# The first and last microseconds of a two-layer block: a weight piece multiplied in fp32, another first root, a second transposing of one chunk, smaller output pieces

## The chip, the cores and the metric

The kernel runs on one core of a Trainium2 chip. Its engines work beside each other: TensorE (PE, with its weight loads shown as PEld), VectorE (DVE), ScalarE (ACT), GpSimd (POOL) and SyncE (SP), which here only issues DMAs. The metric is the device time of one execution in microseconds (us); for the kernel before it is the median of three runs. One further execution was taken with the hardware profiler, and all durations come from that one.

## What is computed

Two layers over 256 tokens of width 1024, all in fp32. Each layer is a half-step feed-forward block, a mixer (a recurrent one in layer 0, an mLSTM in layer 1) and another half-step feed-forward block, each behind an RMS norm that is modulated by a condition vector c. Only the first block's entry and the final norm matter here:

```python
c_act = silu(c)
mod = (c_act @ ada_w[layer] + ada_b[layer]).reshape(1, 3, 3, D_MODEL)
h = rms_norm(x, norm_g[0, 0]) * (1 + mod[:, 0, 1]) + mod[:, 0, 0]
x = x + 0.5 * (1 + mod[:, 0, 2]) * (silu(h @ w_gate) * (h @ w_up)) @ w_down
...
return rms_norm(x, final_norm_g)
```

with `rms_norm(x, g) = x * rsqrt(mean(x * x) + 1e-6) * g`.

## The kernel before

**Layout.** The state x is held transposed, as 8 chunks of 128 channels by 256 tokens. A product has a 128x128 weight tile as its stationary operand and a 128x256 chunk as its moving one. To keep fp32 accuracy at the speed of the narrower type fp32r, each operand is split into a high part (rounded to fp32r) and a low part (the rest), and `multiply` makes three products: high by high, high by low, low by high.

**Weights.** `Weights` brings the weights in pieces of 8 tiles (128x1024, 512 KB) in the order of use. `_piece` (L88) issues a piece's DMA on SP's queue into one of four buffers `wraw`, makes the high part on ScalarE (L96 for the first two pieces, L100 for the others) and the low part on VectorE (L101). A buffer is free for the piece four later when both have read it. `behind` adds order among the instructions of one engine without a wait for data.

**The start (L171 to L212, L298 to L344, L521 to L594).** SP's queue brings x in two blocks of 128 tokens, `xn[:, 0]` and `xn[:, 1]`, then the rows of the modulation matrix in blocks of 512 KB (`ada`), the column vectors `cols` (biases, gains, filter taps) and the weight pieces. ACT's queue brings c. PE spreads c over 128 partitions (L200), ScalarE applies silu (`cact`). VectorE sums the squares of each token (L206). PE transposes x (L211) and ScalarE copies it (L212). `rsqrt_act` (L298) makes the root with ScalarE's Sqrt, which needs a table load, and one correction on VectorE; `spread` (L342) lays it over all partitions as a row. `ada_block` (L223) is one VectorE instruction that multiplies a block with `cact` and sums along the row, which gives 128 values of shift or scale; block 2k and block 2k+1 hold chunk k's shift and scale. b1 (L542) is the fixed part of the scale. Eight transposes (`WARM`, L530) keep PE at work until the first product.

Then the loop over chunks k (L548). Chunks 0 and 1 are modulated by `modulate_chunk` (L400): a VectorE product with scale and root (L404), ScalarE's high part (L406), VectorE's low part (L407). Chunks 2 to 7 are first multiplied by the root three at a time (L563) and then modulated on ScalarE (L566 to L570), the low part on VectorE (L571). For each chunk PE runs through 8 output tiles with gate and up, 16 weight tiles or two pieces, 48 products; results add up in 8 banks of PSUM. The two ada blocks of chunk k+1 are placed in the program behind the first tile of chunk k. A scheduler sets the order on each engine from priorities and from the orders that the kernel adds by hand (`add_manual_dep`, `issue_after`); each engine and each DMA queue then works strictly in its order.

**Beside it.** `dt_weights` (L654) loads a small matrix `wdt` over POOL's queue, for the mixer 200 us later, and splits it (L660, L661).

**The end (L1299 to L1315).** `rsqrt_act` makes the final root of the token sums; PE transposes x back (L1306) into four banks; ScalarE scales the first 128 tokens (L1312) and VectorE the second (L1314), 512 columns at a time, and each result of 256 KB goes out by its own DMA, three on SP's queue and one on ACT's.

Of the kernel before, what the change touches and what calls it, by code (L numbers as in the profile page):

```python
# [11 lines left out]
F32 = mybir.dt.float32  # L12
F32R = mybir.dt.float32r
I32 = mybir.dt.int32
AF = mybir.ActivationFunctionType
ALU = mybir.AluOpType
# [14 lines left out]
    ("ada_b", 6 * 24), ("norm_g", 6 * 8),  # L31
# [32 lines left out]
WARM = 8  # L64
# [8 lines left out]
class Weights:  # L73
# [14 lines left out]
    def _piece(self, i):  # L88
        nc = self.nc
        w = PIECE * P  # L90
        raw = self.raw_pool.tile([P, w], F32, tag="wraw", name=f"wraw{i}")
        nc.sync.dma_start(raw, self.src[i])
        hi, lo = (self.part_pool.tile([P, w], F32R, tag=f"{n}{'abc'[i % 3]}", name=f"{n}{i}") for n in ("whi", "wlo"))
        with self.tc.high_priority(offset=self.ahead):
            if i < 2:
                raw_hi = nc.scalar.copy(hi, raw)  # L96
                if i == 1:
                    self.tc.add_manual_dep(raw_hi.ins, self.first[1].ins.name, NOSYNC, reason="the first input first")
            else:
                raw_hi = nc.scalar.copy(hi, raw)  # L100
            self.last = nc.vector.tensor_tensor(out=lo, in0=raw, in1=hi.bitcast(F32), op=ALU.subtract)  # L101
        if i < 2:
            self.tc.add_manual_dep(self.last.ins, self.first[0].ins.name, NOSYNC, reason="the first input first")
        self.parts[i] = (hi, lo)
        self.splits[i] = (raw_hi, self.last)
        if i:
# [15 lines left out]
    def next(self):  # L122
        i, k = divmod(self.pos, PIECE)
        if k == 0:
            while self.made <= min(i + (self.LEAD if i >= 2 * NF0 - 3 else 1), NTILE // PIECE - 1):
                self._piece(self.made)
                self.made += 1
            self.parts.pop(i - 1, None)
            self.pump(i)
        self.pos += 1  # L130
        hi, lo = self.parts[i]
        return hi[:, k * P:(k + 1) * P], lo[:, k * P:(k + 1) * P]
# [3 lines left out]
def body(ctx: ExitStack, tc: tile.TileContext, a, out, dbg=None):  # L136
# [42 lines left out]
    cols = cst.tile([P, NCOL], F32, name="cols")  # L179
    xs_t = [xall[:, k, :] for k in range(ND)]  # L180
# [16 lines left out]
    cact = cst.tile([P, D], F32, name="cact")  # L197
    for i in range(2):
        b = mm_bank(f"c{i}")
        nc.tensor.matmul(b, ones[0:1, :], crow[:, 512 * i:512 * i + 512], start=True, stop=True)  # L200
        nc.scalar.activation(cact[:, 512 * i:512 * i + 512], b, AF.Silu)

    ss_in = fpool.tile([P, 2], F32, name="ss_in")
    for b in range(2):
        q = fpool.tile([P, D], F32, tag="xsq", name=f"xsq{b}")
        squares = nc.vector.scalar_tensor_tensor(out=q, in0=xn[:, b], scalar=1.0, in1=xn[:, b], op0=ALU.mult,  # L206
                                                 op1=ALU.mult, accum_out=ss_in[:, b:b + 1])
    for k in range(0, ND, 2):
        b = mm_bank(f"xT{k}")
        for i in range(4):  # L210
            nc.tensor.transpose(b[:, i * P:(i + 1) * P], xn[:, i % 2, (k + i // 2) * P:(k + i // 2 + 1) * P], ident)  # L211
        nc.scalar.copy(xall[:, k:k + 2, :], b.rearrange("p (k t) -> p k t", k=2))  # L212
# [68 lines left out]
    def rsqrt_small(v, shape, nm):  # L281
# [11 lines left out]
        nc.vector.scalar_tensor_tensor(out=w, in0=w, scalar=-0.5, in1=v, op0=ALU.mult, op1=ALU.mult)  # L293
        end = nc.vector.scalar_tensor_tensor(out=y, in0=w, scalar=1.5, in1=y, op0=ALU.add, op1=ALU.mult)
# [3 lines left out]
    def rsqrt_act(sums, nm):  # L298

        v = small.tile([P, 2], F32, tag="rs_v", name=f"rsv_{nm}")  # L300
        y = small.tile([P, 2], F32, tag="rs_y", name=f"rsy_{nm}")
        w = small.tile([P, 2], F32, tag="rs_w", name=f"rsw_{nm}")
        nc.vector.tensor_scalar(out=v, in0=sums, scalar1=1.0 / D, scalar2=EPS, op0=ALU.mult, op1=ALU.add)
        nc.scalar.activation(y, sums, AF.Sqrt, bias=eps, scale=1.0 / D)
        nc.vector.reciprocal(y, y)
        nc.vector.tensor_tensor(out=w, in0=y, in1=y, op=ALU.mult)
        nc.vector.scalar_tensor_tensor(out=w, in0=w, scalar=-0.5, in1=v, op0=ALU.mult, op1=ALU.mult)
        return y, nc.vector.scalar_tensor_tensor(out=y, in0=w, scalar=1.5, in1=y, op0=ALU.add, op1=ALU.mult)
# [62 lines left out]
    def multiply(dst, both, start, stop):  # L371

        wh, wl = W.next()
        m = nc.tensor.matmul(dst, wh, both[:, 0, :], start=start, stop=False, skip_group_check=True)  # L374
# [134 lines left out]
    def ffn(s, acc, fp, during=None):  # L509
# [11 lines left out]
        if s == 0:  # L521
# [7 lines left out]
            for _ in range(WARM):  # L529
                nc.tensor.transpose(warm[:, 0:P], xn[:, 0, 0:P], ident)  # L530
            banks = [mm_bank(f"gu0_{j}") if j < 4 else ax_bank(f"gu0_{j}", ("ax", "ax", "p", "q")[j - 4])
                     for j in range(NF0)]
# [7 lines left out]
            b1 = modp.tile([P, 8], F32, tag="gate", name="b1")  # L540
            o, g = COL["ada_b"], COL["norm_g"]
            plus = nc.vector.scalar_tensor_tensor(out=b1, in0=cols[:, o + 8:o + 16], scalar=1.0, in1=cols[:, g:g + 8],  # L542
                                                  op0=ALU.add, op1=ALU.mult)
            tc.add_manual_dep(plus.ins, second_ada.ins.name, NOSYNC, reason="the norm first")
# [3 lines left out]
            for k in range(ND):  # L548
                sc, sh = scales[0][:, k:k + 1], shifts[0][:, k:k + 1]
                gain, bias = cols[:, g + k:g + k + 1], cols[:, o + k:o + k + 1]  # L550
                if k < 2:
# [3 lines left out]
                    chain = modulate_chunk(0, k, pb if k == 0 else rs)  # L555
                    late = chain[2]
                    if k == 1:
                        W.behind(2, 1, chain[0])
                        W.behind(3, 0, chain[1])
# [18 lines left out]
                if k == 0:  # L578
                    W.first = chain
                    nc.scalar.copy(rs, pb)  # L580
                for j in range(NF0):
                    for i in range(2):
                        dst = banks[j][:, i * T:(i + 1) * T]

                        m = multiply(dst, h[k], k == 0 and i == 0, k == ND - 1)
# [4 lines left out]
                        if j == i == 0 and k + 1 < ND:  # L590
                            ada_block(2 * k + 2)
                            ada_block(2 * k + 3)
# [708 lines left out]
    rs, _ = rsqrt_act(sum_tokens(acc, "fin", "mm")[:, 0:2], "fin")  # L1301
# [6 lines left out]
    for lo in (0, 512):  # L1308
        for b in range(2):
            dst, src = res[:, b, lo:lo + 512], banks[2 * (lo // 512) + b]  # L1310
# [4 lines left out]
            (nc.scalar if b == 0 and lo else nc.sync).dma_start(out[b * P:(b + 1) * P, lo:lo + 512], dst)  # L1315
# [108 lines left out]
```

## Time and profile before

| | us |
|---|---|
| median of three runs (lowest, highest) | 1102.14 (1101.68, 1102.78) |
| the profiled execution's own time | 1102.35 |
| its span, first to last record | 1100.6 |
| busy PE, DVE, ACT in the span | 1086.5, 920.1, 642.5 |
| first product of the first block starts | 12.69 |
| last product of the last block starts | 1091.52 |
| first output DMA is issued | 1095.54 |

A line of the order of time gives start and length in us, engine, line of the code, operation, result and operands with their shapes, and in brackets how long the engine had been idle and what ended it. Neighbouring instructions of one kind are merged (x4); the length is then that of the group. A product's record lasts about 0.28 us while the next starts in less than half of that, since products are pipelined. The table of stretches gives busy times of PE, PEld, DVE, ACT and POOL, the granted clock, the share of the 16 DMA engines and GB/s.

### The profile page before, as it was taken

How to read it: one execution, taken by the hardware profiler on the slowest of the kernel's cores; microseconds unless marked ns; L12 is line 12 of the kernel's file. 1: busy time of each engine (PE TensorE's matmuls, PEld its weight loads, DVE VectorE, ACT ScalarE, POOL GpSimd, SP SyncE). 2: the span in 40 equal slices, each digit the busy share in tenths (PEclk: the TensorE clock that was granted, in tenths of full speed). 3: DMA queues.
4: the chain of work that ended last, by engine and by line, in shares of the span. 5: the costliest groups of instructions: out<-in, count | busy, mean ns of one | idle time of the engine just before them, and what ended most of it. 6: DMA issues, size and time to landing. Idle time of an engine off the chain costs nothing.

```text
span 1100.6 us, 23364 instructions
## 1 busy us (share of the span) xinstructions
PE 1086.5 (99%) x9350; PEld 1073.0 (97%) x9350; DVE 920.1 (84%) x1651; ACT 642.5 (58%) x1051; POOL 9.4 (1%) x29
## 2 busy tenths in 40 slices
PE   8999999999999999999999999999999999999997
PEld 7999999999999999999999999999999999999997
DVE  7999998999999899989699988869878868766552
ACT  5665555677986664554454554448776655544452
POOL 0000000000000000000000000010000000000000
PEclk9999999999999999999999999999999999999999
DMA  9989998556845489999848998963432665875551
GB/s 372 335 318 375 393 353 334 192 192 192 287 161 180 155 308 370 351 349 324 279 166 318 347 314 307 316 200 116 151 97 92 198 194 159 269 236 195 195 173 39
DMA packets 74990, 272.34 MB, mean 247 GB/s; under 512 B 8417, under 2 KB 8577, under 8 KB 74882
## 3 DMA queue, kind: packets, MB, share of 16 engines
q1 hardware_dynamic: 74304, 269.49, 70.1%
q8 instruction: 73, 1.20, 0.4%
q0 software_dynamic: 432, 1.10, 0.4%
q14 instruction: 35, 0.29, 0.1%
q10 hardware_dynamic: 146, 0.27, 0.1%
HBM read 269.77 MB, written 1.05 MB: 246 GB/s over the span
## 4 chain that ended last, share of the span: by engine, by line
PE 81%; DVE 13%; ACT 2%; issue 2%; DMA 1%; SPq 0%; DVEq 0%; ACTq 0%
PE gu L375 13%; PE gu L376 13%; PE gu L374 13%; PE od L374 10%; PE od L375 10%; PE od L376 10%; DVE wlo L101 4%; PE gu_f L436 1%; DVE xc L627 1%; PE gu_f L437 1%; PE gu_f L438 1%; DVE ada L232 1%; PE zz L375 1%; PE zz L376 1%; PE zz L374 1%
## 5 line engine op out<-in xcount | busy, mean ns | idle before, releaser
L101 DVE TENSOR_TENSOR wlo<-wraw,whi 128x1024 fp32r<-128x1024 f32 x366 | 445.6, 1221 | 94.4 <-ACT whi L100 92.5
L100 ACT CAST whi<-wraw 128x1024 fp32r<-128x1024 f32 x364 | 380.3, 1050 | 225.5 <-PE od L375 70.8
L375 PE MATMUL gu<-hb,whi 128*128 128x256 f32 x1312 | 361.1, 276 | 0.4 <-DVE hb L571 0.4
L376 PE MATMUL gu<-hb,wlo 128*128 128x256 f32 x1312 | 360.9, 276 | 0.0
L374 PE MATMUL gu<-hb,whi 128*128 128x256 f32 x1312 | 358.6, 277 | 0.8 <-ACT whi L96 0.5
L375 PEld LDWEIGHTS gu<-hb,whi 128*128 128x128 f32 x1312 | 246.3, 188 | 0.8 <-DVE hb L571 0.8
L376 PEld LDWEIGHTS gu<-hb,wlo 128*128 128x128 f32 x1312 | 246.3, 188 | 0.0
L374 PEld LDWEIGHTS gu<-hb,whi 128*128 128x128 f32 x1312 | 244.5, 188 | 1.8 <-ACT whi L96 0.7
L374 PE MATMUL od<-ph,whi 128*128 128x256 f32 x704 | 194.4, 276 | 0.0
L376 PE MATMUL od<-ph,wlo 128*128 128x256 f32 x704 | 194.4, 276 | 0.0
L375 PE MATMUL od<-ph,whi 128*128 128x256 f32 x704 | 194.4, 276 | 0.0
L232 DVE SCALAR_TENSOR_TENSOR ada<-ada,cact 128x1024 f32<-128x1024 f32 x144 | 175.2, 1218 | 0.9 <-DMA ada<-in_adaT_dram 0.9
L375 PEld LDWEIGHTS od<-ph,whi 128*128 128x128 f32 x704 | 132.2, 188 | 0.0
L376 PEld LDWEIGHTS od<-ph,wlo 128*128 128x128 f32 x704 | 132.2, 188 | 0.0
L374 PEld LDWEIGHTS od<-ph,whi 128*128 128x128 f32 x704 | 132.2, 188 | 0.0
L361 ACT CAST ph<-fg 128x256 fp32r<-128x256 f32 x88 | 35.0, 407 | 102.7 <-DVE fg L518 102.5
L362 DVE TENSOR_TENSOR ph<-fg,ph 128x256 fp32r<-128x256 f32 x88 | 36.4, 421 | 11.8 <-ACT ph L361 11.7
L494 DVE SCALAR_TENSOR_TENSOR x<-od,gate,x 128x256 f32<-128x256 f32 x48 | 23.1, 481 | 27.4 <-PE od L376 27.3
L351 ACT ACTIVATE sq_o<-x 128x256 f32<-128x256 f32 x42 | 17.5, 417 | 44.9 <-DVE x L494 44.7
L374 PE MATMUL zz<-hb,whi 128*128 128x256 f32 x128 | 36.2, 282 | 0.0
L376 PE MATMUL zz<-hb,wlo 128*128 128x256 f32 x128 | 36.1, 282 | 0.0
L375 PE MATMUL zz<-hb,whi 128*128 128x256 f32 x128 | 36.1, 282 | 0.0
(412 smaller groups left out, 1950.5 us busy)
## 6 DMA issues: line engine op xcount, KB each, us to landing
wraw<-in_wst_dram SPq DMA_DIRECT2D x366, 512.0 KB, 4.7
ada<-in_adaT_dram SPq DMA_DIRECT2D x144, 512.0 KB, 5.6
xn<-in_x_dram SPq DMA_DIRECT2D x2, 512.0 KB, 3.9
wgr<-in_ml_wg_dram POOLq DMA_DIRECT2D x3, 256.0 KB, 3.1
out_dram<-res SPq DMA_DIRECT2D x3, 256.0 KB, 2.4
out_dram<-res ACTq DMA_DIRECT2D x1, 256.0 KB, 2.8
cols<-in_cols_dram SPq DMA_DIRECT2D x1, 226.0 KB, 7.1
wkr<-in_ml_wkr_dram POOLq DMA_DIRECT2D x1, 128.0 KB, 2.3
```

The costliest lines, as they stand in the source:

```text
L100: raw_hi = nc.scalar.copy(hi, raw)
L101: self.last = nc.vector.tensor_tensor(out=lo, in0=raw, in1=hi.bitcast(F32), op=ALU.subtract)
L232: return nc.vector.scalar_tensor_tensor(out=raw, in0=raw, scalar=1.0, in1=cact, op0=ALU.mult, op1=ALU.mult, accum_out=mods[s][:, m:m + 1])
L351: square = nc.scalar.activation(q, x, AF.Square).ins
L361: nc.scalar.copy(hi, src)
L362: nc.vector.tensor_tensor(out=both[:, 1, :], in0=src, in1=hi.bitcast(F32), op=ALU.subtract)
L374: m = nc.tensor.matmul(dst, wh, both[:, 0, :], start=start, stop=False, skip_group_check=True)
L375: nc.tensor.matmul(dst, wh, both[:, 1, :], start=False, stop=False, skip_group_check=True)
L376: nc.tensor.matmul(dst, wl, both[:, 0, :], start=False, stop=stop, skip_group_check=True)
L436: nc.tensor.matmul(dst, wh, rh, start=(k == 0), stop=False)
L437: nc.tensor.matmul(dst, wh, rl, start=False, stop=False)
L494: nc.vector.scalar_tensor_tensor(out=xs_t[d], in0=dst, scalar=g[:, d:d + 1], in1=xs_t[d], op0=ALU.mult, op1=ALU.add)
```

## The change

- The first weight piece is not split. Its 8 tiles are multiplied as they are, in fp32, with an unsplit chunk 0 (`h0`).
- The first root is made on VectorE by `rsqrt_small` (a guess from the bits and two corrections, eight small instructions, no table). The squares of the second block of tokens are summed half on VectorE, half on ScalarE.
- Chunk 0 is scaled by the root token by token in its untransposed form (`xs0`), transposed again into `x0`, and modulated by ScalarE into `h0`, from which high and low part are then made. The transposing of chunks 6 and 7 moves behind it, and `rs`, the row of roots, is copied after `h0`.
- `cols` comes in two parts: the first 72 columns (gains and the first block's biases) on ACT's queue at the start, the rest on SP's queue in the third round of the loop. b1 is made between the sums of squares.
- Four transposes of the identity stand ahead of the spreading of c; `WARM` is 3 instead of 8.
- Orders by hand: the first two ada blocks behind the root; all later ones in turn, the fourth behind chunk 0's low part and piece 1's split, the fifth and sixth behind chunk 1's low part.
- `wdt` is loaded on SP's queue.
- `rsqrt_act` serves only the end now: Sqrt is traced first, and the correction is made for each half of the tokens by itself, two instructions each.
- The output goes out as pieces of 256, 256 and 512 columns for each half of the tokens: five DMAs on SP's queue, one on ACT's.

```diff
@@ class Weights, _piece
+        if i < WHOLE:
+            self.parts[i] = (raw, None)
+            return
...
-            if i < 2:
-                raw_hi = nc.scalar.copy(hi, raw)
...
+            raw_hi = nc.scalar.copy(hi, raw)
@@ body
+    near = COL["ada_b"] + 24
+    nc.scalar.dma_start(cols[:, 0:near], a["cols"][:, 0:near])
...
+    idle = ax_bank("idle", "q")
+    for _ in range(4):
+        beat = nc.tensor.transpose(idle[:, 0:P], ident, ident)
...
+    for b, lo, hi in ((0, 0, D), (1, 0, 512)):
+        squares = nc.vector.scalar_tensor_tensor(out=q[:, lo:hi], in0=xn[:, b, lo:hi], scalar=1.0,
+                                                 in1=xn[:, b, lo:hi], op0=ALU.mult, op1=ALU.mult,
+                                                 accum_out=ss_in[:, b:b + 1])
+        if b == 0:
+            nc.vector.tensor_scalar(out=ss_in[:, 0:1], in0=ss_in[:, 0:1], scalar1=D * EPS, scalar2=None, op0=ALU.add)
+            plus = nc.vector.scalar_tensor_tensor(out=b1, in0=cols[:, o + 8:o + 16], scalar=1.0, in1=cols[:, g:g + 8],
+                                                  op0=ALU.add, op1=ALU.mult)
+    tc.add_manual_dep(squares.ins, plus.ins.name, NOSYNC, reason="while the input comes")
+    other = nc.scalar.activation(q[:, D:D + 512], xn[:, 1, 512:D], AF.Square, accum_out=ss_in[:, 2:3])
...
@@ rsqrt_act
+        nc.scalar.activation(r, sums, AF.Sqrt, bias=eps, scale=1.0 / D)
+        nc.vector.tensor_scalar(out=v, in0=sums, scalar1=-0.5 / D, scalar2=-0.5 * EPS, op0=ALU.mult, op1=ALU.add)
+        nc.vector.reciprocal(r, r)
+        for b in range(2):
+            one = r[:, b:b + 1]
+            nc.vector.scalar_tensor_tensor(out=w[:, b:b + 1], in0=one, scalar=one, in1=v[:, b:b + 1], op0=ALU.mult,
+                                           op1=ALU.mult)
+            nc.vector.scalar_tensor_tensor(out=y[:, b:b + 1], in0=w[:, b:b + 1], scalar=1.5, in1=one, op0=ALU.add,
+                                           op1=ALU.mult)
@@ multiply
+        if wl is None:
+            return nc.tensor.matmul(dst, wh, both, start=start, stop=stop, skip_group_check=True)
@@ ffn, s == 0
-            y, end = rsqrt_act(acc, "n0")
-            pb = spread(y, "n0", "ax")
+            nc.vector.scalar_tensor_tensor(out=acc[:, 1:2], in0=acc[:, 1:2], scalar=D * EPS, in1=acc[:, 2:3],
+                                           op0=ALU.add, op1=ALU.add)
+            y = rsqrt_small(acc[:, 0:2], [P, 2], "n0", D ** 0.5)
+            end = rsqrt_ends[-1]
+            xs0 = fpool.tile([P, 2, P], F32, name="xs0")
+            for b in range(2):
+                scaled = nc.scalar.activation(xs0[:, b], xn[:, b, 0:P], AF.Copy, scale=y[:, b:b + 1])
...
+            with tc.issue_after(last_in.ins):
+                pb = spread(y, "n0", "ax")
+            x0 = ax_bank("x0", "p")[:, 0:T]
+            for b in range(2):
+                m = nc.tensor.transpose(x0[:, b * P:(b + 1) * P], xs0[:, b], ident)
...
-            tc.add_manual_dep(first_ada.ins, squares.ins.name, NOSYNC, reason="the norm first")
-            tc.add_manual_dep(second_ada.ins, end.ins.name, NOSYNC, reason="the norm first")
-            nc.sync.dma_start(cols, a["cols"])
+            tc.add_manual_dep(first_ada.ins, end.ins.name, NOSYNC, reason="the norm first")
+            tc.add_manual_dep(second_ada.ins, first_ada.ins.name, NOSYNC, reason="in order")
...
+                    with tc.issue_after(copies[-1].ins):
+                        nc.scalar.activation(sh, mods[0][:, 0:1], AF.Identity, bias=bias)
+                        nc.scalar.activation(sc, mods[0][:, 8:9], AF.Identity, bias=b1[:, 0:1], scale=gain)
+                    h0 = fpool.tile([P, T], F32, name="h0")
+                    W.first = late = nc.scalar.activation(h0, x0, AF.Identity, bias=sh, scale=sc)
+                    W.behind(1, 0, late)
+                    W.behind(2, 0, late)
+                    hi = nc.scalar.copy(h[0][:, 0, :], h0)
...
+                if k == 2:
+                    nc.sync.dma_start(cols[:, near:], a["cols"][:, near:])
...
-                        m = multiply(dst, h[k], k == 0 and i == 0, k == ND - 1)
+                        m = multiply(dst, h0 if W.pos < WHOLE * PIECE else h[k], k == 0 and i == 0, k == ND - 1)
...
@@ dt_weights
-        nc.gpsimd.dma_start(wdt, a["wdt"])
+        nc.sync.dma_start(wdt, a["wdt"])
@@ the end
-    for lo in (0, 512):
+    for lo, hi in ((0, 256), (256, 512), (512, 1024)):
...
-            (nc.scalar if b == 0 and lo else nc.sync).dma_start(out[b * P:(b + 1) * P, lo:lo + 512], dst)
+            (nc.scalar if b == 0 and lo == 512 else nc.sync).dma_start(out[b * P:(b + 1) * P, lo:hi], dst)
```

More of the change, by code (lines that the diff above doesn't have):

```diff
@@ L197, in body @@
     cact = cst.tile([P, D], F32, name="cact")
+    idle = ax_bank("idle", "q")
+    for _ in range(4):
+        beat = nc.tensor.transpose(idle[:, 0:P], ident, ident)
+    spreads, silus = [], []
     for i in range(2):
         b = mm_bank(f"c{i}")
[L200 to L207, printed above, removed]
@@ L208, in body @@
-    for k in range(0, ND, 2):
+        spreads.append(nc.tensor.matmul(b, ones[0:1, :], crow[:, 512 * i:512 * i + 512], start=True, stop=True))
+        silus.append(nc.scalar.activation(cact[:, 512 * i:512 * i + 512], b, AF.Silu))
+    tc.add_manual_dep(spreads[0].ins, beat.ins.name, NOSYNC, reason="the clock first")
+    ss_in = fpool.tile([P, 3], F32, name="ss_in")
+    q = fpool.tile([P, D + 512], F32, name="xsq")
+    b1 = modp.tile([P, 8], F32, tag="gate", name="b1")
+    o, g = COL["ada_b"], COL["norm_g"]
@@ L209, in body, with transposes @@
+    tc.add_manual_dep(squares.ins, plus.ins.name, NOSYNC, reason="while the input comes")
+    other = nc.scalar.activation(q[:, D:D + 512], xn[:, 1, 512:D], AF.Square, accum_out=ss_in[:, 2:3])
+    tc.add_manual_dep(other.ins, silus[0].ins.name, NOSYNC, reason="one table")
+    tc.add_manual_dep(silus[1].ins, other.ins.name, NOSYNC, reason="the norm first")
+    copies = [silus[1]]
+    def transposes(k):
         b = mm_bank(f"xT{k}")
         for i in range(4):
-            nc.tensor.transpose(b[:, i * P:(i + 1) * P], xn[:, i % 2, (k + i // 2) * P:(k + i // 2 + 1) * P], ident)
@@ L212, in body @@
-        nc.scalar.copy(xall[:, k:k + 2, :], b.rearrange("p (k t) -> p k t", k=2))
+            last = nc.tensor.transpose(b[:, i * P:(i + 1) * P], xn[:, i % 2, (k + i // 2) * P:(k + i // 2 + 1) * P], ident)
+        copies.append(nc.scalar.copy(xall[:, k:k + 2, :], b.rearrange("p (k t) -> p k t", k=2)))
+        tc.add_manual_dep(copies[-1].ins, copies[-2].ins.name, NOSYNC, reason="in order")
+        return last
+    for k in (0, 2, 4):
+        last_in = transposes(k)
     tri = cst.tile([P, P], F32, name="tri")
@@ L300, in rsqrt_act @@
         v = small.tile([P, 2], F32, tag="rs_v", name=f"rsv_{nm}")
+        r = small.tile([P, 2], F32, tag="rs_r", name=f"rsr_{nm}", bufs=1)
         y = small.tile([P, 2], F32, tag="rs_y", name=f"rsy_{nm}")
         w = small.tile([P, 2], F32, tag="rs_w", name=f"rsw_{nm}")
[L303 to L308, printed above, removed]
+        nc.scalar.activation(r, sums, AF.Sqrt, bias=eps, scale=1.0 / D)
[7 more added lines that the diff above has]
+                                           op1=ALU.mult)
+        return y
     def sum_tokens(acc, nm, tag):
@@ L590, in ffn @@
                         if j == i == 0 and k + 1 < ND:
-                            ada_block(2 * k + 2)
-                            ada_block(2 * k + 3)
+                            for b in (2 * k + 2, 2 * k + 3):
+                                block = ada_block(b)
+                                tc.add_manual_dep(block.ins, second_ada.ins.name, NOSYNC, reason="in order")
+                                second_ada = block
+                                if b == 3:
+                                    tc.add_manual_dep(block.ins, low.ins.name, NOSYNC, reason="the nearer chunk first")
+                                    tc.add_manual_dep(block.ins, W.splits[1][1].ins.name, NOSYNC,
+                                                      reason="the nearer piece first")
+                                if k == 1:
+                                    tc.add_manual_dep(block.ins, late.ins.name, NOSYNC, reason="the nearer chunk first")
             for j in range(NF0):
```

55 lines of the change are left out of this document (28 added, 27 removed).

## The prediction

> **What bounds the kernel now.** I read the page first, then the table of busy time by stretches, then the order of time of the first 60 us and the last 20.
>
> ```profile
> span 1100.6 us, 23364 instructions
> PE 1086.5 (99%) x9350; PEld 1073.0 (97%) x9350; DVE 920.1 (84%) x1651; ACT 642.5 (58%) x1051; POOL 9.4 (1%) x29
> ```
> ```profile
> 0.00:12.70 12.70, 9.93 (x33) 6.78 (x33) 7.00 (x18) 7.80 (x13) 2.08 (x12) 1.00 0.85 326
> 20.00:30.00 10.00, 9.67 (x82) 9.28 (x81) 9.64 (x14) 5.43 (x10) 0.00 (x0) 1.00 1.03 409
> 30.00:40.00 10.00, 9.73 (x82) 9.33 (x82) 9.19 (x14) 6.57 (x11) 0.00 (x0) 1.00 1.02 399
> 100.00:200.00 100.00, 99.99 (x881) 99.78 (x880) 93.10 (x152) 50.30 (x69) 0.98 (x3) 1.00 0.94 348
> ```
>
> TensorE is busy for 99% of the span, and the change leaves all but its first and last few microseconds alone. What can be won lies before the first product, in stalls between the first chunks, and behind the last product. The second table gives, for each stretch, its length, then busy time of PE, PEld, DVE, ACT and POOL, the clock, the DMA share and GB/s. From 20 to 40 us three things are full at once: PE, VectorE (9.64 and 9.19 of 10) and the DMA engines (share 1.03 and 1.02). So the reader must ask whether an earlier first product survives that stretch.
>
> ```profile
> 12.69 0.74 PE L374 MATMUL gu<-hb,whi 128*128 128x256 f32 x4
> 13.89 0.39 PE L374 MATMUL gu<-hb,whi 128*128 128x256 f32 x1 [0.47 <-ACT whi L96]
> 25.10 0.72 PE L374 MATMUL gu<-hb,whi 128*128 128x256 f32 x4
> 26.06 0.39 PE L375 MATMUL gu<-hb,whi 128*128 128x256 f32 x1 [0.23 <-DVE hb L571]
> 36.84 0.74 PE L374 MATMUL gu<-hb,whi 128*128 128x256 f32 x4
> 37.79 0.39 PE L375 MATMUL gu<-hb,whi 128*128 128x256 f32 x1 [0.21 <-DVE hb L571]
> 38.02 0.28 PE L376 MATMUL gu<-hb,wlo 128*128 128x256 f32 x1
> ```
>
> PE stops at chunk 0, at chunk 2 (25 us) and last at chunk 4 (37 us), each time after four products, until VectorE has delivered. Where nothing holds it, from 100 to 200 us, PE starts 881 products in 100 us, one every 0.1135, so a chunk of 48 takes 5.45. With the sixth product at 38.02, chunk 4 starts in effect at 37.45. No gap follows up to the end of chunk 7. The front is thus worth what it moves **that wait**.
>
> ```profile
> 8.01 1.22 DVE L232 SCALAR_TENSOR_TENSOR ada<-ada,cact 128x1024 f32<-128x1024 f32 x1 [0.86 <-DMA ada<-in_adaT_dram]
> 9.84 0.15 DVE L308 SCALAR_TENSOR_TENSOR rsy_n<-rsw_n,rsy_n 128x2 f32<-128x2 f32 x1
> 9.91 1.22 DVE L232 SCALAR_TENSOR_TENSOR ada<-ada,cact 128x1024 f32<-128x1024 f32 x1
> 11.05 1.04 ACT L96 CAST whi<-wraw 128x1024 fp32r<-128x1024 f32 x1 [0.30 <-DMA wraw<-in_wst_dram]
> 12.12 1.23 DVE L101 TENSOR_TENSOR wlo<-wraw,whi 128x1024 fp32r<-128x1024 f32 x1
> 13.87 1.23 DVE L101 TENSOR_TENSOR wlo<-wraw,whi 128x1024 fp32r<-128x1024 f32 x1
> 15.01 1.22 DVE L232 SCALAR_TENSOR_TENSOR ada<-ada,cact 128x1024 f32<-128x1024 f32 x1
> 16.16 1.22 DVE L232 SCALAR_TENSOR_TENSOR ada<-ada,cact 128x1024 f32<-128x1024 f32 x1
> 16.17 1.05 ACT L100 CAST whi<-wraw 128x1024 fp32r<-128x1024 f32 x1 [2.33 <-DMA wraw<-in_wst_dram]
> 42.75 0.43 DVE L571 TENSOR_TENSOR hb<-ht,hb 128x256 fp32r<-128x256 f32 x1 [0.45 <-ACT ht L570]
> 53.61 0.42 DVE L571 TENSOR_TENSOR hb<-ht,hb 128x256 fp32r<-128x256 f32 x1 [0.45 <-ACT ht L570]
> ```
>
> From 15.01 on VectorE runs one chain of ada blocks, low parts of weights and low parts of inputs, each 1024-wide instruction 1.14 after the one before. Two chunks of it take 53.61 - 42.75 = 10.86, or 5.43 per chunk: PE's own pace, so it can't catch up what it starts late. I therefore date the change by the end of ada block 3, 16.16 + 1.14 = 17.30.
>
> **The change part by part.**
>
> ```profile
> 5.71 1.23 DVE L206 SCALAR_TENSOR_TENSOR xsq<-xn 128x1024 f32<-128x1024 f32 x1 [0.18 <-DMA xn<-in_x_dram]
> 7.03 1.28 ACT L304 ACT_TABLE_LOAD   x1 [0.32 <-DVE xsq L206]
> 1094.43 0.16 DVE L307 SCALAR_TENSOR_TENSOR rsw_fin<-rsw_fin,rsv_fin 128x2 f32<-128x2 f32 x1
> 1094.63 0.16 DVE L308 SCALAR_TENSOR_TENSOR rsy_fin<-rsw_fin,rsy_fin 128x2 f32<-128x2 f32 x1
> ```
>
> *Root.* The second block of x is there at 5.7. Its squares are halved between VectorE and ScalarE: 0.65 instead of 1.23, to about 6.5. The root's table load (1.28) goes. One sum and eight small instructions take its place at 0.20 each (1094.43 to 1094.63), 1.8: y at 8.4 against 9.84 + 0.15 = 9.99. ScalarE scales two 128x128 blocks, PE transposes them while ada 0 and 1, now behind the root, run on VectorE: 8.4 + 2 x 1.14 = 10.7 against 11.05. Scale, then one 128x256 activation, and the first product comes at about 11.9 against 12.69. The spread over partitions, the copies of x and the second transposing lie under those two ada blocks and cost nothing; without that cover they would be about 1.5.
>
> *First piece whole.* It removes one high part (1.04 of ScalarE) and one low part (1.23 of VectorE) and three-pass products of 8 tiles, 24 x 0.1135 = 2.7. It adds 8 products in fp32.
>
> ```profile
> 755.26 1.03 PE L1078 MATMUL q<-xc,we 128*128 128x256 f32 x4
> 2.32 3.75 PE L200 MATMUL c<-crow,ones 1*128 1x512 f32 x4 [2.32 <-DMA crow<-in_c_dram]
> 6.00 3.68 PE L211 MATMUL xT<-ident,xn 128*128 128x128 f32 x16
> ```
>
> L1078 is called 16 times and leaves 32 records, so an fp32 product is two. Four records in 1.03, the last of about 0.38, give 0.22 between starts, 0.43 a tile, 3.5 for the piece: 0.8 more than before. At the start PE is slower: the 512-wide ones of L200 come 0.9 apart, or 0.45 for 256 columns and 0.9 a tile, 7.2 for the piece. I take 3.5, since the products from 13.89 on were at 0.1135, but keep 7.2. With 3.5, chunk 0 ends at 11.9 + 3.5 + 2.7 = 18.1, sooner than the 19.0 at which chunk 1 began, and VectorE decides.
>
> The Trainium skill, page "TensorE: Matmul & The Clock Gate", section "Part 4: PE-mode transpose", says that the full clock doesn't engage for transposes, which speaks against the four idle transposes put ahead of the first product. The trace agrees so far: 16 transposes in a row keep 0.22 apart for 3.7 us, twice the 0.1135 of a 256-wide product later. By the rule the sum would use 7.2, without it 3.5.
>
> *VectorE's chain.* Ada 1 ends at 10.7. Chunk 0's activation, its high part and the high part of piece 1 are then ScalarE's, to about 13.2. VectorE's low part of chunk 0 (0.35) hides under them; low part of piece 1 to 14.3 or 14.4; ada 2 and 3 to 16.6 or 16.7. Do they land in time? Pieces 0 and 2 land at 11.05 and 16.17; four transfers of 512 KB between make 1.28 each, so ada 2 and 3 land near 13.6 and 14.9. The rest of cols and wdt, 0.25 MB at 400 GB/s, are no longer ahead: 0.6 sooner. They do. If ada 2 is placed ahead of the low parts, VectorE waits for its landing and comes out at 16.5 to 16.8. So ada 3 ends 0.5 to 0.85 earlier.
>
> ```profile
> 27.97 1.06 ACT L100 CAST whi<-wraw 128x1024 fp32r<-128x1024 f32 x1 [0.50 <-DMA wraw<-in_wst_dram]
> 29.46 0.39 ACT L566 ACTIVATE scale<-mod,b,cols 128x1 f32<-128x1 f32 x1 [0.43 <-DVE ada L232]
> ```
>
> *DMA further on.* Piece 6 is waited for, and behind its cast stands chunk 3's scale with 0.43 to spare. By then the rest of cols, and probably wdt, have been moved as before, so this landing hardly moves: a gain over 0.43 is cut here to between 0.43 and 1.0. Piece 4's transfer needs the buffer of piece 0, now read by PE to 15.4 instead of by VectorE to 13.35; it and what follows on SP's queue issue 2 us later, hidden by ada 4 and 5, still moving up to about 19. I take **0.5** for the front.
>
> *Queues.* The near columns go from SP to ACT's queue ahead of the first table load, which has 1.7 us to spare; SP's weights issue 0.5 earlier. wdt goes from POOL's queue to SP's, one issue of 0.4 among waits of SP, taken as nothing.
>
> *End.*
>
> ```profile
> 1094.83 1.26 ACT L1312 ACTIVATE res<-fin,rsy_fin 128x512 f32<-128x512 f32 x2 [0.82 <-DVE rsy_fin L308]
> 1094.83 1.41 DVE L1314 TENSOR_SCALAR res<-fin,rsy_fin 128x512 f32<-128x512 f32 x2
> 1095.54 1.32 SPq L1315 DMA_DIRECT2D out_dram<-res  x3
> 1096.12 0.38 ACTq L1315 DMA_DIRECT2D out_dram<-res  x1
> 1096.50:1097.00 0.50, 0.00 (x0) 0.00 (x0) 0.00 (x0) 0.00 (x0) 0.00 (x0) 1.00 1.02 377
> ```
>
> The root's first half is ready one small instruction sooner (0.2), its second half one later. A quarter-width piece takes between half and all of 0.68, so SP's first issue comes at about 1095.1 instead of 1095.54. But SP then issues five times at 0.44, the last at 1096.9 instead of 1096.4. The output moves at 377 GB/s, 2.8 us for 1.05 MB, so an earlier start counts while the small pieces keep that rate, and a late last issue if they don't: -0.5 to +0.5. Nearest to the full rate I take **-0.2**.
>
> Sum: -0.7. The profiled execution took 1102.35 us, its span 1100.6; that gives 1101.65. The median of the runs is 0.21 under it: 1101.4.
>
> **The rivals.**
> (a) *VectorE is ordered by landings.* Ada 3 can't end before 14.3 + 1.14 = 15.4, 1.9 earlier, and piece 6 doesn't hold chunk 3. With -0.2: 1100.0. For it: VectorE idles some 2 us between 10.7 and 13.2. Against: piece 6.
> (b) *Slow clock over the whole first piece.* 11.9 + 7.2 + 2.7 + 3 x 5.45 = 38.1 for chunk 4, 0.7 behind 37.45; if it warms half way, 36.3, and VectorE decides again. Full price with the end: 1102.6. By the page's rule this one comes true.
> (c) *The near columns come late.*
>
> ```profile
> cols<-in_cols_dram SPq DMA_DIRECT2D x1, 226.0 KB, 7.1
> wdt<-in_wdt_dram POOLq DMA_DIRECT2D x1, 64.0 KB, 5.6
> ```
>
> VectorE's b1 reads them and stands ahead of the second squares, the root and everything after. It costs from a landing after 5.7 on. At cols' 7.1 from an issue at 1.4 it is 8.5: y at 11.0, ada 1 at 13.3, ada 3 at 18.1, 0.85 late: slower, 1102.8. Against: they are 36 KB, of 226.
> (d) *wdt's cast stops ScalarE.* Issued on SP behind ada 5 (about 10) it lands 5.6 to 8 later, up to 18. If the cast stands before chunk 1's high part, wanted at 17.4, ScalarE and the chain wait 0.5 to 2: slower, 1103.4 at most. It decides only if the cast is ordered there; before, it ran at 10.4, already landed.
> (e) *Nothing moves*, since three resources are full: 1102.1.
>
> **How the numbers follow.** Forecast 0.48, (a) 0.18, (b) 0.10, (c) 0.10, (d) 0.08, (e) 0.06. The forecast's own range, with both ends of the front and the end piece, is 1100.6 to 1102.2; with (a) to (d) I reach from 1099.8 to 1103.0. A measurement of this kernel tells about 0.2%, 2.2 us, from no change. Faster by more than that is most of (a), with the better end piece: 0.13. Slower by more is the worst of (c) and (d) with the worse end piece: 0.07. Within it: 0.80.
>
> **What would show it.** First product near 11.9; its eight tiles in 3.5; the second ada pair ending at 16.4 to 16.8; the gap at chunk 4 still there, near 37.3; the first output issue 0.4 earlier. A second table load in the start, VectorE idle before b1, ScalarE idle before wdt's cast, or PE's fp32 records 0.45 apart would prove me wrong, as would any shift of stages after 60 us.

## The result, and where the time came from

The changed kernel takes 1116.59 us (median of four runs, 1116.38 to 1118.02) against 1102.46 for the kernel before in the same runs: 1.27% slower, ratio 1.0127 with a 95% interval of 1.0115 to 1.0140. The prediction had 1101.4 and a range from 1099.8 to 1103.0. The profiled execution took 1116.38, its span 1114.7.

Three points that both kernels have cut the span into a front, a middle and an end: the first product of the first down projection, and the scaling of x by the final gain ahead of the output. First the rows of the kernel before, in order of time, then those of the changed one. (The spans in the traces are 1100.63 and 1114.67; the table uses them.)

```profile
135.46 0.28 PE L374 MATMUL od<-ph,whi 128*128 128x256 f32 x1
...
1092.80 0.51 ACT L1304 ACTIVATE x<-x,cols 128x256 f32<-128x256 f32 x1
```
```profile
span 1114.7 us, 23366 instructions
...
135.56 0.28 PE L406 MATMUL od<-ph,whi 128*128 128x256 f32 x1
...
1106.64 0.51 ACT L1367 ACTIVATE x<-x,cols 128x256 f32<-128x256 f32 x1
```

| part of the span, us | before | after | difference |
|---|---|---|---|
| front, up to the first down product | 135.46 | 135.56 | +0.10 |
| middle | 957.34 | 971.08 | +13.74 |
| end, from the last scaling on | 7.83 | 8.03 | +0.20 |

The front and the end, where nearly all the edits lie, cost 0.30 together. The other 13.74 come from the middle, in which no product was edited. PE is busy for 99% of the span before and after; so its products themselves must have become slower. The groups of instructions with their shapes kept apart (count, busy us, mean ns of one record) say which, first before, then after:

```profile
L375 PE MATMUL gu<-hb,whi 128*128 128x256 f32 x1312 | 361.1, 276 | 0.4 <-DVE hb L571 0.4
L374 PE MATMUL od<-ph,whi 128*128 128x256 f32 x704 | 194.4, 276 | 0.0
L374 PE MATMUL od<-yb,whi 128*128 128x256 f32 x128 | 35.3, 276 | 0.0
```
```profile
L407 PE MATMUL gu<-hb,whi 128*128 128x256 f32 x1304 | 359.6, 276 | 0.0
L407 PE MATMUL od<-ph,whi 128*128 128x256 f32 x704 | 197.6, 281 | 0.0
L407 PE MATMUL od<-yb,whi 128*128 128x256 f32 x128 | 35.9, 281 | 0.0
```

Products of one shape, with the same weights tiles: gate and up products, with hb as moving operand, still take 276 ns, those with ph and yb 281. (Some small groups with hb have longer records, zz for one 282, but the same before and after.) Records overlap, so the price is read from how many are under way in a stretch that PE fills; 500 to 550 us is such a stretch of down products, before and after (the number behind PE's busy time is the count):

```profile
500.00:550.00 50.00, 50.00 (x444) 50.00 (x443) 39.34 (x59) 25.30 (x33) 1.06 (x2) 1.00 0.87 302
```
```profile
500.00:550.00 50.00, 50.00 (x425) 50.00 (x425) 39.64 (x57) 23.06 (x30) 0.00 (x0) 1.00 0.87 307
```

The granted clock is 1.00 in both, the DMA share 0.87 in both, and PE never idles; but there is one product for every 50/425 = 0.1176 us instead of every 50/444 = 0.1126. That is 5.0 ns, 4.4%. (The counts hold two or three products that were under way at the start, so from start to start it is 0.118 and 0.113.) All products of `out_project` have ph, yb, ysb or ylb as moving operand, three passes of 704, 128, 64 and 64: 2880. 13.74/2880 = 4.8 ns each, and the whole loss is accounted for.

Does PE lose this to the traffic of the others, who read and write the same memory? The last down projection answers. Near its end VectorE, ScalarE and GpSimd do nothing and the DMA engines have a share of 0.00, before and after:

```profile
1086.00:1091.00 5.00, 5.00 (x47) 5.00 (x46) 0.00 (x0) 0.00 (x0) 0.00 (x0) 1.00 0.00 0
```
```profile
1100.00:1105.00 5.00, 5.00 (x45) 5.00 (x44) 0.00 (x0) 0.00 (x0) 0.00 (x0) 1.00 0.00 0
```

Even there 45 products stand against 47, one every 0.118 us from start to start against 0.113. So the loss needs no other engine and no DMA: it arises among what PE itself reads and writes.

What do ph, yb, ysb and ylb share, and hb not? They are allocated behind the pool `small`, hb ahead of it. And one line of the change, which the shortened diff ahead of the prediction leaves out, adds a tile to `small`:

```diff
     def rsqrt_act(sums, nm):
         v = small.tile([P, 2], F32, tag="rs_v", name=f"rsv_{nm}")
+        r = small.tile([P, 2], F32, tag="rs_r", name=f"rsr_{nm}", bufs=1)
         y = small.tile([P, 2], F32, tag="rs_y", name=f"rsy_{nm}")
```

Eight bytes per partition that take a slot of 32. In the compiled kernels' addresses every later pool starts 32 bytes further on (modulo 512): ph, yb, ysb and ylb at byte 352 of 512 instead of 320, while hb stays at 320, the high weights at 384 and the low ones at 256. The code before even speaks of such places: `partp` is laid out with `PLACES` modulo 512 (L143 to L150), and each stage opens with an unread tile, `spad` (L154) or `pad{s}` (L1274).

### The profile page after: what moved, and what is told of

Same layout as the page of the kernel before. It is cut to its first block, busy times and chain, and to the rows that moved or that the text cites. A ratio compares the mean times of both kernels' runs of the same rounds, so it can differ in the third digit from the quotient of the medians.

```text
span 1114.7 us, 23366 instructions
## 1 busy us (share of the span) xinstructions
PE 1100.4 (99%) x9343; PEld 1086.7 (97%) x9343; DVE 919.1 (82%) x1654; ACT 641.4 (58%) x1055; POOL 8.8 (1%) x28
## 4 chain that ended last, share of the span: by engine, by line
PE 83%; DVE 12%; ACT 2%; issue 2%; DMA 1%; POOL 0%; DVEq 0%; ACTq 0%; SPq 0%; POOLq 0%
PE gu L408 13%; PE gu L407 13%; PE gu L406 13%; PE od L408 10%; PE od L407 10%; PE od L406 10%; DVE wlo L100 4%; PE gu_f L468 1%; DVE xc L690 1%; PE gu_f L470 1%; PE gu_f L469 1%; DMA wraw<-in_wst_dram 1%; PE zz L407 1%; PE zz L408 1%; PE zz L406 1%
## 5 line engine op out<-in xcount | busy, mean ns | idle before, releaser
L407 PE MATMUL od<-ph,whi 128*128 128x256 f32 x704 | 197.6, 281 | 0.0
L408 PE MATMUL od<-ph,wlo 128*128 128x256 f32 x704 | 197.6, 281 | 0.0
L406 PE MATMUL od<-ph,whi 128*128 128x256 f32 x704 | 197.5, 281 | 0.0
L549 ACT ACTIVATE fg<-gu 128x256 f32<-128x256 f32 x82 | 30.8, 376 | 13.3 <-PE gu L408 13.3
L406 PE MATMUL zz<-hb,whi 128*128 128x256 f32 x128 | 36.1, 282 | 0.0
```

Source lines behind the costliest of these rows:

```text
L407: nc.tensor.matmul(dst, wh, both[:, 1, :], start=False, stop=False, skip_group_check=True)
L408: nc.tensor.matmul(dst, wl, both[:, 0, :], start=False, stop=stop, skip_group_check=True)
L549: nc.scalar.activation(g, b[:, 0:T], AF.Silu)
```

## The experiments

**Is it the 32 bytes?** The changed kernel with an unread pad made 32 bytes smaller, and the kernel before with the same pad made 32 or 64 bytes larger and nothing else changed. The theory: the place of the moving operand. The rivals: the edits of the front and the end themselves, or a loss of 64-byte alignment.

```diff
-    small.tile([P, 96], F32, name="spad", bufs=1)
+    small.tile([P, 88], F32, name="spad", bufs=1)     # changed kernel, e1
+    small.tile([P, 104], F32, name="spad", bufs=1)    # kernel before, e2
+    small.tile([P, 112], F32, name="spad", bufs=1)    # kernel before, e3
```

> The changed kernel with 32 bytes taken off the filler tile ahead of the pools that come after it, so that all later tiles stand where they stood in the kernel before. Theory A (the new tile rs_r moved every later tile by 32 bytes, and products whose moving operand stands there take 4.5 ns longer each; some 2880 of them make 13 us): od products back at 276 ns mean instead of 281, time 1101 to 1104 us. Rival B (the new orders at the start or the DMA order make the products slower): time stays at 1116 to 1117 us, od at 281 ns. Rival C (the first 30 us lose it): time falls by less than 3 us.

> The kernel before with 32 bytes added to the same filler tile and nothing else. Theory A: od products at 281 ns, time 1114 to 1117 us. Rivals B and C: 1102 us, od at 276 ns.

> The kernel before with 64 bytes added to the filler tile. Theory A1 (what counts is whether the moving operand starts on a multiple of 64 bytes): 1102 us, od at 276 ns. Theory A2 (what counts is its place within 512 bytes against the weights' place, or any shift): another time than 1102, 1106 us or more, od over 277 ns.

Measured: e1 1103.31, ratio to before 1.0004 (0.9995 to 1.0013). e2 1116.58, ratio 1.0126 (1.0111 to 1.0142). e3 1118.43, ratio 1.0141 (1.0127 to 1.0155). The groups of e1, then of e2, then of e3:

```profile
L407 PE MATMUL od<-ph,whi 128*128 128x256 f32 x704 | 194.3, 276 | 0.0
```
```profile
L375 PE MATMUL od<-ph,whi 128*128 128x256 f32 x704 | 197.6, 281 | 0.0
```
```profile
L375 PE MATMUL od<-ph,whi 128*128 128x256 f32 x704 | 198.5, 282 | 0.0
```

The loss goes with the pad alone, in both directions, and so the other edits aren't its cause. At 64 bytes it is larger, not gone: alignment to 64 falls.

**Does it go with the products?** The pads of the four feed-forward stages alone, 32 and then 512 bytes larger; the mixing stages' yb, ysb and ylb stay.

```diff
-                fp.tile([P, 56 if s in (2, 5) else 48], F32, name=f"pad{s}", bufs=1)
+                fp.tile([P, 64 if s in (2, 5) else 56], F32, name=f"pad{s}", bufs=1)     # e4
+                fp.tile([P, 184 if s in (2, 5) else 176], F32, name=f"pad{s}", bufs=1)   # e5
```

> The kernel before with 32 bytes added inside the four feed-forward pools alone, so that only ph moves: 2112 of the 2880 od products. Theory A in proportion: 2112 x 4.5 ns = 9.5 us, time 1111 to 1113 us, od<-ph at 281 ns, od<-yb, ysb and ylb at 276 ns. If it is another tile behind the filler (temporaries, x as loaded), 1102 us.

> The kernel before with 512 bytes added inside the four feed-forward pools alone; the run with 64 bytes has shown that a multiple of 64 is not what counts. Theory A2 (what counts is the place within 512 bytes): od<-ph at 276 ns, 1102 to 1103 us. Rival (any shift from the tuned place costs, or the distance between tiles): od<-ph at 280 ns or more, 1111 us or more.

Measured: e4 1112.76, ratio 1.0090 (1.0077 to 1.0104). e5, one run, 1102.08 against 1102.62. e4's groups:

```profile
L375 PE MATMUL od<-ph,whi 128*128 128x256 f32 x704 | 197.6, 281 | 0.0
L374 PE MATMUL od<-yb,whi 128*128 128x256 f32 x128 | 35.3, 276 | 0.0
```

Only the moved tiles pay: (1112.76 - 1102.66)/2112 = 4.8 ns for each of 3 x 704 products. A move by 512 bytes costs nothing, so the place within 512 counts, and not that the tile lies further on.

**The place itself, or its distance to the weights?** In e6 a 32-byte tile goes ahead of the weight buffers: the weights and all tiles behind them, ph among them, move together, and hb, which lies ahead, stays. In e9 it goes ahead of all of them.

```diff
+    partp.tile([P, 8], F32, name="pad_first", bufs=1)    # e6, ahead of the weight buffers
+    cst.tile([P, 8], F32, name="pad_all")                # e9, ahead of all tiles
```

> The kernel before with 32 bytes added ahead of the split weights, so that the weights (stationary) and ph (moving) both move by 32 and the chunks hb (moving) stay. If the place of the moving operand relative to the weights counts: od stays at 276 ns, gu<-hb rises to about 280 ns; some 5400 products of hb make 20 to 25 us, 1123 to 1128 us. If the moving operand's own place within 512 bytes counts: od at 281 ns, gu at 276 ns, 1115 to 1117 us. If the weights' own place counts: both rise, 1135 us or more.

> The kernel before with one 32-byte tile ahead of everything else, so that the inputs hb, the split weights and ph, yb, ysb, ylb all move by 32 bytes together and their distances stay. If the distance between moving operand and weights decides: 1102.6 (1101.7 to 1103.9), every product at 276 ns as before. If the place of the moving operand itself decides: all 3936 gu products and the 2880 od products go to 280 or more, 6816 x 4.5 ns = 31 us slower, 1133. If the place of the weights itself decides, the same or more.

Measured, one run each: e6 1120.41 against 1102.62, e9 1103.03 against 1102.66. The time of e6 fell between the numbers that had been put down for two theories; its groups decide. First e6, then e9:

```profile
L376 PE MATMUL gu<-hb,whi 128*128 128x256 f32 x1312 | 366.9, 281 | 0.3 <-DVE hb L572 0.2
L377 PE MATMUL gu<-hb,wlo 128*128 128x256 f32 x1312 | 365.3, 279 | 0.0
L376 PE MATMUL od<-ph,whi 128*128 128x256 f32 x704 | 194.3, 276 | 0.0
```
```profile
L376 PE MATMUL gu<-hb,whi 128*128 128x256 f32 x1312 | 361.2, 276 | 0.4 <-DVE hb L572 0.4
L376 PE MATMUL od<-ph,whi 128*128 128x256 f32 x704 | 194.3, 276 | 0.0
```

In e6 the picture is turned round. ph, at the place that cost 281 ns in e2, is back at 276 because the weights moved with it; hb, which didn't move, has become slow, because the weights moved away from it. The stretches show it too: from 40 to 100 us, all gate and up products, there are 511 instead of 532, and from 140 to 160, down products, 179 in both. 60/511 - 60/532 is 4.6 ns. Added up from start to start, the 3936 gate and up products take 16.5 us longer than before; the rest of the loss, 17.8 us in all, is in the smaller groups of hb. (One group of hb doesn't pay: the 288 products gu_f, 258 wide, have records of 282 to 285 ns in e6 and of 283 to 288 before. No run explains that.) When everything moves (e9), nothing is slow. So the **distance between the moving operand and the weights** decides. The theory of the moving operand's own place, with which the runs began, falls. Strictly, e6 moved all that lies behind the weights as well; that the weights are the partner, and not another of these tiles, rests on this, that a product reads nothing else there, and that the loss is the same while nothing but PE works.

**With which period?** ph moved by 256 (e10) and by 128 bytes (e12), weights in place.

```diff
+                fp.tile([P, 120 if s in (2, 5) else 112], F32, name=f"pad{s}", bufs=1)   # e10
+                fp.tile([P, 88 if s in (2, 5) else 80], F32, name=f"pad{s}", bufs=1)     # e12
```

> The kernel before with ph, yb, ysb and ylb of the feed-forward stages moved by 256 bytes instead of 32 (the mixing stages' tiles stay). If the price hangs on the distance within 256 bytes: 1102.6, od<-ph at 276 ns. If it hangs on the distance within 512 bytes and grows with it as from 32 to 64: 280 to 285 ns, 2112 x 4.5 to 9 ns = 9.5 to 19 us slower, 1112 to 1122.

> The kernel before with ph, yb, ysb and ylb of the feed-forward stages moved by 128 bytes. High and low weights lie 128 bytes apart within 512 (384 and 256) and their products take the same 276 ns with one moving tile, so if only the distance within 128 bytes decides: 1102.6, od<-ph at 276 ns. If the distance within 256 decides: od<-ph at 280 ns or more, 1112 or later.

Measured, one run each: e10 1102.63 against 1102.66; e12 1113.89 against 1102.37. The groups of e10, then of e12:

```profile
L375 PE MATMUL od<-ph,whi 128*128 128x256 f32 x704 | 194.6, 276 | 0.0
```
```profile
L375 PE MATMUL od<-ph,whi 128*128 128x256 f32 x704 | 199.2, 283 | 0.0
L374 PE MATMUL od<-ph,whi 128*128 128x256 f32 x704 | 196.4, 279 | 0.0
L376 PE MATMUL od<-ph,wlo 128*128 128x256 f32 x704 | 196.1, 279 | 0.0
```

256 bytes are free, 128 are not: of the moves tried, those by a multiple of 256 cost nothing, those by 32, 64 and 128 cost 4.8 to 5.5 ns a product on the mean of the passes. (High and low weights lie 128 apart and are equally fast with one moving tile, and a move by 128 only swaps the two distances. So it can't be the distance to the product's own weights alone; which weight load it is that meets the moving stream wasn't tried.)

**What is left of the change?** With the pad mended (e1), the front and the end remain. e7 gives the unsplit first piece a buffer of its own, e8 also moves ScalarE's copies of x behind the nearer chunk's scaling, e11 also goes back to output pieces of 512 columns. All three keep e1's pad, and the new buffer is laid so that the tiles behind it stay where they were.

```diff
+        raw = (self.own.tile([P, w], F32, name=f"wraw{i}") if i < WHOLE else       # e7
+               self.raw_pool.tile([P, w], F32, tag="wraw", name=f"wraw{i}"))
...
+            tc.add_manual_dep(copies[-1].ins, scaled.ins.name, NOSYNC, reason="the nearer chunk first")     # e8
...
+                    tc.add_manual_dep(copies[-1].ins, late.ins.name, NOSYNC, reason="the nearer chunk first")
...
-    for lo, hi in ((0, 256), (256, 512), (512, 1024)):                              # e11
+    for lo, hi in ((0, 512), (512, 1024)):
```

> The changed kernel with the 32 bytes taken off, and with a buffer of its own for the first piece (the squares are written into xr instead, to make room), so that the fifth piece's DMA no longer waits until PE has read the first. Theory F1 (the fifth piece's late landing, 21.7 us, holds ScalarE and so chunk 2, and costs what the earlier start gives): SP issues the fifth piece before 13 us, the cast of it no longer waits 2.6 us, chunk 2 begins without the 0.7 and 0.8 us gaps, time 0.5 to 1.2 us under the run with the 32 bytes alone, near 1102.2. Rival F2 (the bytes ahead in the DMA engines set the landing, not the issue): no change, 1103.3.

> As the run before, and ScalarE's copies of chunks 4 and 5 ordered behind the scaling of the token blocks, those of chunks 6 and 7 behind chunk 0's activation. Theory: the first product comes at 11.9 to 12.1 instead of 12.9, as forecast; VectorE's chain hangs on ada's landings and hardly moves, so the time falls by 0 to 0.5 us against the run before. Rival (the first product decides): 1 us less.

> The changed kernel with the pad 32 bytes smaller, piece 0 in a buffer of its own, the nearer chunk's scaling ahead of the copies on ScalarE, and the output in pieces of 512 again (four issues, not six), with the two-part root kept. If the six issues cost what the traces show (the span ends 0.26 later after the sums of the tokens although y is 0.26 sooner): 0.3 to 0.5 under the same kernel with six pieces, 1101.8, ratio 0.9993 against before, last issue on SP about 0.8 sooner. If the smaller pieces helped: 0.2 to 0.5 later, 1102.5.

| | median | ratio to before | front | end |
|---|---|---|---|---|
| before | 1102.62 and 1102.66 | 1 | 135.46 | 7.83 |
| e1, pad mended | 1103.31 | 1.0004 (0.9995 to 1.0013) | 136.05 | 8.02 |
| e7, own buffer | 1102.86 | 1.0002 (0.9992 to 1.0011) | 135.82 | 8.00 |
| e8, and copies later | 1102.20 | 0.9997 (0.9989 to 1.0006) | 135.21 | 8.00 |
| e11, and old pieces | 1102.01 | 0.9996 (0.9987 to 1.0005) | 135.57 | 7.47 |

Front and end are those of the first table, from each one's profiled execution. None of the four can be told from the kernel before by its time; the best of them, e11, doesn't beat it beyond the interval. Nor can they be told from each other by it: e7 is 0.45 under e1, e8 0.66 under e7, e11 0.19 under e8, and neighbouring intervals overlap. Of what was expected, the traces show this. In e7 the fifth piece is issued at 9.78 and its cast waits 0.48 instead of 2.65, as theory F1 had it; but the two gaps of chunk 2 stay (0.41 and 0.69), against F1. In e8 the first product comes at 11.94, as expected, and the 0.66 lie between the theory's 0.5 and the rival's 1. In e11 SP's last issue ends 0.87 sooner after the final scaling and the end is 0.53 shorter than in e8, as the theory of the six issues had it.

How far do fronts differ with no edit? In the eight profiled executions with the old front (the kernel before, e2 to e5, e9, e10 and e12) the first down product starts between 134.90 and 135.74, 0.84 apart. So the fronts of the table, one execution each, show no gain. The ends are steadier: 7.83 to 7.85 in these eight, 8.00 to 8.03 in the four executions with the new end.

## Why the prediction was wrong, step by step

**The step that failed** stands in its first part: TensorE "is busy for 99% of the span, and the change leaves all but its first and last few microseconds alone". The first half was read from the page and is right. The second counts the edited instructions alone. The new tile `rs_r` was part of the change and was costed nowhere; it moved the four tiles that 2880 products read as moving operand. The prediction had no term for addresses, and of the 14.0 us by which the span grew 13.7 lie there. It had named "any shift of stages after 60 us" as what would prove it wrong, and that is what came. No rival held it: all five were about the front.

**The front: 0.5 forecast, nothing measured.** A second step failed here, the one that dates the front by the end of ada block 3 and takes the order behind it as it was. The rows of the changed kernel:

```profile
9.65 0.70 ACT L563 ACTIVATE xs<-xn,rsy_n 128x128 f32<-128x128 f32 x2
11.20 0.59 ACT L232 COPY x<-xT 128x512 f32<-128x512 f32 x1 [0.85 <-PE xT L231]
12.29 0.56 ACT L598 ACTIVATE h<-x,shift,scale 128x256 f32<-128x256 f32 x1
12.91 3.72 PE L405 MATMUL gu<-h,wraw 128*128 128x256 f32 x16 [1.41 <-ACT h L598]
15.54 1.22 DVE L257 SCALAR_TENSOR_TENSOR ada<-ada,cact 128x1024 f32<-128x1024 f32 x1
15.65 1.33 SPq L93 DMA_DIRECT2D wraw<-in_wst_dram  x2
21.69 1.06 ACT L99 CAST whi<-wraw 128x1024 fp32r<-128x1024 f32 x1 [2.65 <-DMA wraw<-in_wst_dram]
23.92 0.95 DVE L616 TENSOR_TENSOR xr<-x,rs 128x768 f32<-128x768 f32 x1
24.97 0.60 ACT L621 ACTIVATE hb<-xr,shift,scale 128x256 fp32r<-128x256 f32 x1 [1.75 <-DVE xr L616]
25.62 0.74 PE L406 MATMUL gu<-hb,whi 128*128 128x256 f32 x4 [0.79 <-ACT hb L621]
27.05 0.74 PE L406 MATMUL gu<-hb,whi 128*128 128x256 f32 x4 [0.69 <-ACT whi L99]
```

- *First product at 11.9: 12.91.* The copies of x were said to "lie under those two ada blocks and cost nothing". They do, for VectorE; but ScalarE has to do them, and it took them ahead of the scaling (9.65, a microsecond after the root's end at 8.63) and of shift and scale, behind the copy at 11.20. In e8, with the copies behind, the first product starts at 11.94:

```profile
11.94 3.72 PE L409 MATMUL gu<-h,wraw 128*128 128x256 f32 x16
```

- *Eight fp32 tiles in 3.5:* sixteen records from 12.91, the next product at 16.28: 3.4. Right in this execution and in three of the four others with the piece (rival (b) is taken up below).
- *Ada 3 ends 0.5 to 0.85 earlier:* 15.54 + 1.14 = 16.68 against 17.30. Right for these two executions; in the eight with the old front it ends between 16.81 and 17.64.
- *Piece 4's late transfer "hidden by ada 4 and 5":* ScalarE doesn't hide it. It is issued at 15.65, and ScalarE idles for 2.65 before its high part at 21.69. VectorE loses only 0.28 by it, and in e7, where piece 0 doesn't hold a buffer, the same cast waits 0.48. Yet chunk 2 isn't ready any sooner there:

```profile
20.08 1.05 ACT L100 CAST whi<-wraw 128x1024 fp32r<-128x1024 f32 x1 [0.48 <-DMA wraw<-in_wst_dram]
24.12 0.95 DVE L619 TENSOR_TENSOR xr<-x,rs 128x768 f32<-128x768 f32 x1
25.16 0.60 ACT L624 ACTIVATE hb<-xr,shift,scale 128x256 fp32r<-128x256 f32 x1 [1.68 <-DVE xr L619]
```

- *The order behind ada 3,* which the prediction took as unchanged. The root's product `xr`, without which chunk 2 can't be modulated, stands on VectorE right behind chunk 1's low part in the kernel before:

```profile
19.61 0.95 DVE L563 TENSOR_TENSOR xr<-x,rs 128x768 f32<-128x768 f32 x1
```

In the changed kernel two ada blocks and two low parts of weights come first, four instructions of 1.14 each. From the start of ada 3 to that of `xr` it is 19.61 - 16.16 = 3.45 before, 23.92 - 15.54 = 8.38 after and 24.12 - 16.10 = 8.02 in e7: the four instructions make 4.6, and most of the remaining 0.36 is the late piece. ScalarE waits 1.75 for `xr`, and PE stops at chunk 2, first for ScalarE's hb and then for a high part that ScalarE makes behind it. Which of the orders by hand moved `xr` was not tried.
- *The stop at chunk 4 stays:* it is gone. Having lost its time at chunk 2, PE doesn't stop again, and the first down product comes at 135.56, as before. In the eight executions with the old front it starts 119.2 to 119.3 behind the start of ada 3, in e3 and e9 too, whose first products run at half the later rate for over 1 us. So ada 3 dates the old front, and not the first product, as the prediction said. In the five with the new front the same distance is 119.7 to 120.4: what ada 3 gained went into the stops at chunk 2.

**The end: -0.2 forecast, +0.20 measured,** within its -0.5 to +0.5. The changed kernel, then e11:

```profile
1108.41 1.42 ACT L1375 ACTIVATE res<-fin,rsy_fin 128x256 f32<-128x256 f32 x3 [0.76 <-DVE rsy_fin L336]
1108.91 2.42 SPq L1378 DMA_DIRECT2D out_dram<-res  x5
1109.86 0.36 ACTq L1378 DMA_DIRECT2D out_dram<-res  x1
```
```profile
1093.27 0.51 ACT L1373 ACTIVATE x<-x,cols 128x256 f32<-128x256 f32 x1
1095.76 1.32 SPq L1384 DMA_DIRECT2D out_dram<-res  x3
1096.34 0.35 ACTq L1384 DMA_DIRECT2D out_dram<-res  x1
```

Counted from the scaling by the final gain, SP's first issue comes after 2.27 (1108.91 - 1106.64) instead of 2.74 (1095.54 - 1092.80): 0.47 sooner, as forecast. But SP then issues until 4.69, in e11 with three issues until 3.81, before until 4.06. Of the two ends that the prediction kept, the late last issue was the true one. With the old pieces the new root's gain is kept: the end takes 7.47 in e11 against 7.83 before and 8.00 in e8. The small pieces thus cost 0.5, the root brings 0.4.

**The rivals.** (a) and (d) didn't come: ada 3 wasn't early by 1.9, and wdt was loaded only at 71.0, far behind the front. (c) came in small: VectorE idled 0.41 for the near columns, which were there at 5.95 and not by 5.7, and the root ended at 8.63, 0.2 behind the forecast. VectorE's idle time before b1 was also among the signs that the prediction named against itself. (e) came for the front in its time, +0.10, but not by its reason: the order on VectorE held it, not three full resources. (b), the slow clock over the first piece, came in part, in one of the five profiled executions with the piece. This is the profile of e1, a stretch with its clock (the column behind the busy times) and the first piece:

```profile
12.70:20.00 7.30, 7.01 (x32) 6.09 (x33) 7.17 (x12) 4.24 (x7) 0.00 (x0) 0.77 1.03 408
```
```profile
12.99 5.41 PE L405 MATMUL gu<-h,wraw 128*128 128x256 f32 x16 [1.41 <-ACT h L598]
```

5.41 instead of 3.72, at a mean clock of 0.77: half clock for (1 - 0.77) x 2 x 7.3 = 3.4 us. The front of e1 is the latest of the table, 136.05, half a microsecond behind that of the changed kernel, whose profile has 1.00 there with the same 1.41 of idle time ahead; with one execution of each, this isn't parted from the spread of 0.8. The piece's 3.5 were 3.4 in four executions and 5.1 in e1 (next product at 18.05). The 7.2 that the prediction gave to a start at which transposes don't bring the full clock came in none, though the transposes of x and the idle ones ran ahead of the piece in all five.

## What to carry to other kernels

Read a diff for its tiles as well as for its instructions: a new tag in a shared pool moves every pool behind it, and a padding tile that nobody reads tells that someone cared where the next one lies. Where PE is the bound and a stage slows without waiting, compare the mean record and the starts per stretch by moving operand: groups that differ in nothing but the tile's name point to its place. Put new small tiles behind the operands of products, or take their bytes from a pad; then look whether an edit on a critical engine has put its helpers (copies, casts, DMA issues) ahead of the work that it was to hasten, and whether what the next stage needs, like `xr` here, has slipped behind work that can wait.

## What the runs showed of the hardware

A product with a 128x256 fp32r moving operand starts every 0.113 us or, on the mean of the three passes, 4 to 5% later, by the distance in bytes between moving operand and weights, at the same clock, DMA share and shape:

| moved against the weights by | mean record, ns | run |
|---|---|---|
| 0 (also with both moved by 32) | 276 | before, e6's ph, e9 |
| 32 | 281 | after, e2, e4 |
| -32 (weights moved, hb not) | 279 to 282 | e6's hb |
| 64 | 282 | e3 |
| 128 | 279 to 283 | e12 |
| 256, 512 | 276 | e10, e5 |

The loss is there while no other engine and no DMA works (45 products against 47 in 5 us). That weight loads run beside the products (PEld is busy for 97% of the span) makes it likely that the two reads meet in the memory, but this is argued: no run took the loads away. Of other widths only the 258-wide gu_f was seen, which didn't pay in e6; other types were not tried.

The clock can fall around a short idle time. After the same 1.41 us without a product, one execution had the first piece at full clock and another at half of it for 3.4 us. The Trainium skill, page "TensorE: Matmul & The Clock Gate", section "Part 1: The HAM clock gate (the "warmup" mystery)", says that activity is judged in windows of about 3.4 us that run freely and don't start with the work. The two executions agree with that as far as they go: the same gap is charged or not, and the fall lasted one window.

The clock column can mislead at the very start. In e9 it shows 1.00 throughout, yet 12 products fill the first 2.7 us and 42 the next 4.6, one every 0.22 and then every 0.11:

```profile
12.70:15.40 2.70, 2.70 (x12) 2.31 (x12) 2.57 (x4) 1.29 (x3) 0.00 (x0) 1.00 1.03 419
15.40:20.00 4.60, 4.60 (x42) 4.60 (x41) 4.57 (x10) 2.51 (x3) 0.00 (x0) 1.00 1.03 410
```

The rate doubles at 15.4 as at a change of clock that the column doesn't show. At the start, the clock is better read from the spacing of the products.
